# Up projection of a hybrid encoder layer: product 2 with joined matmuls of 512 columns and a sum of two halves

## The chip, the cores and the metric

The kernel runs on one core of a Trainium2 chip. The metric is the device time of one execution in microseconds (us); less is better.

## What is computed

One layer of a hybrid bidirectional encoder for 512 tokens of width 2048, all in float32. The part that matters here is the gated MLP at its end:

```python
xn = rms_norm(x, ffn_norm_g[l])
up = jnp.einsum("bsd,df->bsf", xn, w_up[l])          # 2048 -> 2 x 5632
up = depthwise_conv(up, ffn_dw_w[l], ffn_dw_b[l])    # width 3 over the tokens
gate, val = jnp.split(up, 2, axis=-1)
x = x + jnp.einsum("bsf,fd->bsd", jax.nn.silu(gate) * val, w_down[l])
```

Ahead of it stand an input projection with a convolution branch and an attention branch, and an output projection; behind it a final RMS norm.

## The kernel before

**Stages.** In order of time: the input projection with both branches (lines 374, 158 to 161), the output projection (158 to 161), the up projection (727 to 776), the down projection (882) and the final norm. This document is about the up projection, which runs from about 690 to 1555 us of the span. It is a loop of 44 rounds (`NF`), one for each block of 128 gate columns and 128 value columns.

**Seven products.** A round does not multiply the four quarters of its weights (A11, A12, A21, A22) with the two halves of the contraction and the two halves of the tokens in eight products, but forms sums of quarters and of activations beforehand and makes seven products of half the tokens (a Strassen-like scheme in the Winograd form). The products are named by a number `c` from 0 to 6 and run in the order `TURN = (3, 2, 4, 5, 1, 0, 6)`. So product 2 is the second to run. Its result is the one that is added to both halves of the value columns.

**Two parts of each number.** To keep float32's accuracy with the faster float32r matmuls, each operand is split in a high part (rounded) and a low part (the rest). A product of weights `hi`, `lo` and activations `mh`, `ml` is hi·mh + hi·ml + lo·mh, each over eight blocks of contraction (`U = 8`). In `comb[c][k]` a tile of 512 columns holds `mh` in its first 256 columns (`H = 256`) and `ml` in the other 256.

- Joined form (all products but 2): one matmul of `hi` with all 512 columns gives hi·mh in the first half of the PSUM bank and hi·ml in the second; one of `lo` with 256 columns adds lo·mh to the first half. That makes 8 matmuls of 512 and 8 of 256 columns. The two halves must be added afterwards, which `folded` does: ScalarE (ACT) copies the second half to SBUF, VectorE (DVE) adds the first. `FIRST` names the products that run their high part ahead of the low one; the others run the low part first.
- Product 2 uses `mm3` instead: three matmuls of 256 columns for each block, all into the first half of the bank. That makes 24 matmuls of 256 columns, and one copy by ACT (line 763) takes the result out.

**Banks.** Products 3, 4 and 1 accumulate one after another in the bank `pa`; ACT copies its state to other banks in between (`copied`, line 752). Product 4 can begin to add only when the copy of `pa` after product 3 is done; product 2, which has a bank `pc_` of its own, runs meanwhile.

**Around it.** For each product ACT rounds the raw weights to `whi` (line 131) and DVE makes `wlo` (line 132). Weights are made three products ahead (`AHEAD`), with four buffers for `whi` and `wlo` (`NW`) and nine for the raw weights (`NR`), which come over the SyncE (SP) queue; two of the seven weights in a round get a second quarter added by a transfer issued by GpSimd (POOL, line 687), two by DVE (lines 697 and 699). DVE and ACT also do the convolution of the round before: line 785 on ACT, two taps for the gate and two for the value on DVE (786 and 787), the silu (804) and the product (805). All instructions of an engine run in the order that a priority scheduler wrote out when the kernel was built; within a product, `pin` keeps the first matmul of a block in program order.

Of the kernel before, what the change touches and what calls it, by code (L numbers as in the profile page):

```python
# [12 lines left out]
AF = mybir.ActivationFunctionType  # L13
# [3 lines left out]
P = 128  # L17
D = 2048
S = 512
# [15 lines left out]
U = 8  # L35
# [5 lines left out]
H = S // 2  # L41
# [10 lines left out]
NEG = -1.0e30  # L52

TURN = (3, 2, 4, 5, 1, 0, 6)
FIRST = (3, 5, 0)
TURN2 = (3, 0, 4, 1, 2, 6, 5)
Q = D // 2 // S
TAIL = 4
# [16 lines left out]
def layer(ctx: ExitStack, tc: tile.TileContext, xT, xn, w_0, w_in, w_out, w_up, w_down, par, tab, g3, out):  # L75
    nc = tc.nc
# [8 lines left out]
    @contextmanager  # L85
    def shifted(by):

        at = tc.cur_priority
        tc.cur_priority = max(at + by, 0)
        yield  # L90
        tc.cur_priority = at + (tc.cur_priority - max(at + by, 0))

    def t2(name, dt=F32):
        return tp.tile([P, S], dt, tag="t2k", name=name)
# [23 lines left out]
    ps = psm.tile([P, S], F32, tag="mm", name="warm")  # L118
# [5 lines left out]
    def raw_unit(src, n):  # L124
        raw = t4([P, U * P], "raw")
        return raw, nc.sync.dma_start(raw[:, :n], src)

    def parts(raw, n):
        hi = wpool.tile([P, U * P], F32R, tag="whi", name="whi", bufs=NW)
        lo = wpool.tile([P, U * P], F32R, tag="wlo", name="wlo", bufs=NW)  # L130
        i = nc.scalar.activation(hi[:, :n], raw[:, :n], AF.Copy)  # L131
        j = nc.vector.tensor_sub(lo[:, :n], raw[:, :n], hi[:, :n].bitcast(F32))  # L132
        with tc.issue_after(j.ins), shifted(600):
            for _ in range(min(len(taps), TAPS)):
                taps.pop(0)()
        return hi, lo, i, j
# [3 lines left out]
        return parts(raw_unit(src, n)[0], n)[:2]  # L140

    tight, taps = [], []

    def mm3(ps, w, wk, mh, ml, start, stop, more=False):
        hi, lo = w[:2]
        a = slice(wk * P, (wk + 1) * P)
        i = nc.tensor.matmul(ps, hi[:, a], mh, start=start, stop=False, skip_group_check=more)  # L147
        if tight:
            pin(i)
        nc.tensor.matmul(ps, hi[:, a], ml, start=False, stop=False, skip_group_check=more)  # L150
        return nc.tensor.matmul(ps, lo[:, a], mh, start=False, stop=stop, skip_group_check=more)  # L151


    def group(ps, ws, ms, first, last):

# [10 lines left out]
    def tick(behind):  # L166
        for todo in (steps, asteps):
            while todo:
                try:
                    with tc.issue_after(behind.ins):  # L170
                        next(todo[0])
                    break
                except StopIteration:
                    todo.pop(0)
# [5 lines left out]
    def weights():  # L180
        at = weights.at
        weights.at += 1
        for i in range(at, min(at + 1 + FAR, len(plan))):
            if i in sums:
                sums.pop(i)()
        while len(made) < min(at + 1 + AHEAD, len(plan)):
            made.append(plan[len(made)]())
        return made[at]
# [85 lines left out]
    pin = tc.keep_in_program_order  # L274
# [33 lines left out]
    for u in range(2):  # L308
        raw, i = raw_unit(w_in[NC_ + 1, :, u * U * P:(u + 1) * U * P], U * P)
        pin(i)  # L310
        for t in range(2 * u, 2 * u + 2):
            for i in range(2):
                x = t4([P, D // 2], "xn")
                pin(nc.sync.dma_start(x, xn[t * P:(t + 1) * P, i * D // 2:(i + 1) * D // 2]))
                if t == 2 * u and i == 0:
                    w = parts(raw, U * P)
# [8 lines left out]
    for step in ORDER:  # L325
        i = next(a_ if step == "a" else q_)
# [242 lines left out]
    p, n = -1, 0  # L569
# [50 lines left out]
    comb = [[] for _ in range(7)]  # L620
# [104 lines left out]
    pd_, pb, pc_ = (psm.tile([P, S], F32, tag="mm", name="pu") for _ in range(3))  # L725
# [3 lines left out]
    def up(f, done):  # L729

        def product(c, ps, more):
            hi, lo = wt = weights()
            if c == 2:
                for k in range(U):
                    m = comb[c][k]
                    i = mm3(ps[:, :H], wt, k, m[:, :H], m[:, H:], k == 0, k == U - 1)
            else:
                turns = [(part, n, k) for part, n in ((lo, H), (hi, S))[::-1 if c in FIRST else 1]
                         for k in range(U)]
                if f == 0 and c == 3:  # L740
                    turns.sort(key=lambda a: a[2])
                for j, (part, n, k) in enumerate(turns):
                    i = nc.tensor.matmul(ps[:, :n], part[:, k * P:(k + 1) * P], comb[c][k][:, :n],  # L743
                                         start=j == 0 and not more, stop=j == 2 * U - 1, skip_group_check=more)
                    if j == 0 and tight:
                        pin(i)
            tick(i)
            done(TURN.index(c), i)

        def copied(to, ps):  # L750
            with shifted(-100):
                nc.scalar.activation(to, ps, AF.Copy)  # L752

        def folded(to, ps):
            nc.scalar.activation(to, ps[..., H:], AF.Copy)
            add(to, to, ps[..., :H])  # L756

        product(3, pa, False)
        tight[:] = [1] * (f > 0)
        copied(pd_, pa)  # L760
        product(2, pc_, False)
        w = t2("w")[:, :H]
        nc.scalar.activation(w, pc_[:, :H], AF.Copy)
        product(4, pa, True)
        copied(pe, pa)
        product(5, pd_, True)
        g = t2("g")
        folded(g[:, :H], pd_)
        product(1, pa, True)
        copied(pb, pa)  # L770
        product(0, pe, True)
        v = t2("vl")
        by = v.rearrange("p (i t) -> p i t", i=2)
        folded(by[:, 1], pa)
        folded(by[:, 0], pe)
        add(by, by, w.unsqueeze(1).broadcast_to([P, 2, H]))
        product(6, pb, True)
        folded(g[:, H:], pb)
        return g, v
# [14 lines left out]
    def hidden(f, done):  # L794
        g, v = up(f, done)

        def finish():
            nc.vector.tensor_mul(g, g, rstd2[0])
            a = conv3(g, f)
            yield  # L800
            nc.vector.tensor_mul(v, v, rstd2[0])
            b = conv3(v, NF + f)
            yield
            nc.scalar.activation(a, a, AF.Silu)
            nc.vector.tensor_mul(a, a, b)
            if f < NF - KEEP:
                nc.sync.dma_start(hd[f], a)
            else:
                hs[f] = a

        if f == NF - 1:
            steps.append(finish())
        else:
            for _ in finish():
                pass
# [47 lines left out]
    def four(first):  # L863

        if first:
            b = psa.tile([P, 2, S], F32, tag="sc", name="pd2")
            return [b[:, 0], b[:, 1]] + [psa.tile([P, S], F32, tag="tr", name="pd", bufs=2) for _ in range(2)]
        return [psm.tile([P, S], F32, tag="mm", name="pd") for _ in range(3)] + [psa.tile([P, S], F32, tag="po",
                                                                                         name="pd")]
# [108 lines left out]
    a = four(True)  # L978
# [18 lines left out]
    a = four(True)  # L997
# [74 lines left out]
```

## Time and profile before

| what | value |
|---|---|
| time, median of 3 runs | 1985.71 us (1985.69 to 1985.72) |
| time of the profiled execution | 1985.57 us |
| its span, first to last instruction | 1983.8 us |
| mean granted TensorE clock | 0.999 |
| 132 copies of a bank by ACT (line 752), mean | 580 ns |
| 573 splits by ACT (line 131) and by DVE (line 132), mean | 1058 and 1222 ns |

In the rows of the profile PE is TensorE's matmuls, PEld its weight loads, L743 is line 743 of the kernel before. A row of the timeline gives the start (us from the span's start), the time, engine, line, operation, output and inputs, tile sizes, how many were merged in the row, and in brackets the idle time before it with what ended it. A row of groups gives the count, then the busy time in us, the mean of one in ns, and the idle time in front. A row of waits gives who waited for whom, the us in total, how often, and the longest. Matmuls overlap: the next starts before the one before has ended.

### The profile page before, as it was taken

What the parts mean: (1) busy time and instruction counts of PE and PEld (TensorE: products, weight loads), DVE (VectorE), ACT (ScalarE), POOL (GpSimd) and SP (SyncE); (2) the same over time, 40 slices, a digit from 0 to 9 for tenths busy, and PEclk for the clock granted to TensorE, in tenths of its full rate; (3) what the DMA queues carried; (4) which work ended last, traced back from release to release, by engine and by line L of the source; (5) the groups of instructions that cost most, each with busy time, mean ns of one, the idle gap of its engine ahead of it and who ended that gap; (6) DMA issues with size and microseconds to landing.
All of it is one profiled execution on the core that took longest, in us unless ns stands there. A gap on an engine that the chain in (4) does not pass through costs nothing.

```text
span 1983.8 us, 28536 instructions
## 1 busy us (share of the span) xinstructions
PE 1969.9 (99%) x10525; PEld 1687.1 (85%) x10525; DVE 1602.7 (81%) x2318; ACT 1098.5 (55%) x1726; POOL 226.0 (11%) x310
## 2 busy tenths in 40 slices
PE   9999999999999999999999999999999999999998
PEld 7888888888788888989899898989898888888886
DVE  5987688788547888888888888888888898886765
ACT  7244424448525676666666666656666644554654
POOL 0111111111001111111111111111110400000000
PEclk9999999999999999999999999999999999999999
DMA  9776777676858889999999999999986977666663
GB/s 367 192 195 178 186 184 190 181 188 189 261 151 212 207 228 273 248 261 250 260 260 246 263 244 266 241 270 241 268 228 182 357 257 229 220 215 195 192 198 122
DMA packets 141821, 451.04 MB, mean 227 GB/s; under 512 B 15088, under 2 KB 23536, under 8 KB 140272
## 3 DMA queue, kind: packets, MB, share of 16 engines
q1 hardware_dynamic: 88880, 293.46, 43.8%
q0 software_dynamic: 42624, 148.92, 35.9%
q10 hardware_dynamic: 10176, 6.83, 1.1%
q8 instruction: 83, 1.36, 0.3%
q14 instruction: 58, 0.48, 0.1%
HBM read 430.27 MB, written 111.15 MB: 273 GB/s over the span
## 4 chain that ended last, share of the span: by engine, by line
PE 93%; DVE 3%; ACT 2%; issue 1%; DMA 1%; ACTq 0%; DVEq 0%
PE pu L743 37%; PE pd L882 21%; PE pj L161 6%; PE pj L158 6%; PE pj L159 6%; PE po L158 3%; PE po L161 3%; PE po L159 3%; PE pu L151 2%; PE pu L150 2%; PE pu L147 2%; PE po L530 1%; PE trp L516 1%; ACT s L506 1%; PE pj L374 1%
## 5 line engine op out<-in xcount | busy, mean ns | idle before, releaser
L131 ACT ACTIVATE whi<-raw 128x1024 fp32r<-128x1024 f32 x573 | 601.7, 1058 | 561.5 <-PE pj L159 171.7
L132 DVE TENSOR_TENSOR wlo<-raw,whi 128x1024 fp32r<-128x1024 f32 x573 | 696.4, 1222 | 253.8 <-ACT whi L131 209.1
L743 PE MATMUL pu<-xc,whi 128*128 128x512 f32 x2112 | 505.6, 391 | 0.1
L743 PEld LDWEIGHTS pu<-xc,whi 128*128 128x128 f32 x2112 | 388.2, 188 | 75.3 <-DVE xc L626 0.3
L882 PE MATMUL pd<-whi,ho 128*128 128x512 f32 x1232 | 305.1, 389 | 0.1
L743 PEld LDWEIGHTS pu<-xc,wlo 128*128 128x128 f32 x2112 | 274.4, 191 | 10.3
L743 PE MATMUL pu<-xc,wlo 128*128 128x256 f32 x2112 | 282.3, 283 | 0.0
L882 PEld LDWEIGHTS pd<-whi,ho 128*128 128x128 f32 x1232 | 231.2, 188 | 48.6 <-DVE vl L756 0.5
L158 PE MATMUL pj<-xh,whi 128*128 128x512 f32 x608 | 241.3, 397 | 0.0
L159 PE MATMUL pj<-xl,whi 128*128 128x512 f32 x608 | 237.4, 390 | 0.0
L400 DVE SCALAR_TENSOR_TENSOR y<-ch,prm,y 128x500 f32<-128x500 f32 (+14 forms) x240 | 177.2, 742 | 5.1
L882 PE MATMUL pd<-wlo,ho 128*128 128x512 f32 x616 | 165.1, 389 | 0.0
L161 PE MATMUL pj<-xh,wlo 128*128 128x512 f32 x608 | 151.0, 390 | 0.0
L752 ACT ACTIVATE pu<-pu 128x512 f32<-128x512 f32 x132 | 76.5, 580 | 121.7 <-PE pu L743 121.5
L158 PEld LDWEIGHTS pj<-xh,whi 128*128 128x128 f32 x608 | 114.1, 188 | 26.3 <-issue 3.6
L882 PEld LDWEIGHTS pd<-wlo,ho 128*128 128x128 f32 x616 | 115.7, 188 | 24.0
L161 PEld LDWEIGHTS pj<-xh,wlo 128*128 128x128 f32 x608 | 114.1, 188 | 23.6
L159 PEld LDWEIGHTS pj<-xl,whi 128*128 128x128 f32 x608 | 114.3, 188 | 23.0 <-issue 0.2
L213 POOL DMA_DIRECT2D ws<-in_w_down x88 | 79.7, 905 | 372.4 <-DMA raw<-in_w_up 130.9
L687 POOL DMA_DIRECT2D raw<-in_w_up x88 | 78.0, 887 | 280.2 <-DVE wlo L132 152.6
L147 PE MATMUL pu<-xc,whi 128*128 128x256 f32 x352 | 99.6, 283 | 0.0
L150 PE MATMUL pu<-xc,whi 128*128 128x256 f32 x352 | 99.6, 283 | 0.0
(190 smaller groups left out, 2318.4 us busy)
## 6 DMA issues: line engine op xcount, KB each, us to landing
raw<-in_w_up SPq DMA_DIRECT2D x220, 512.0 KB, 5.4
ws<-in_w_down POOLq DMA_DIRECT2D x132, 512.0 KB, 6.2
raw<-in_w_up POOLq DMA_DIRECT2D x88, 512.0 KB, 7.6
raw<-ws SPq DMA_DIRECT2D x88, 512.0 KB, 4.3
raw<-in_w_in SPq DMA_DIRECT2D x76, 512.0 KB, 5.1
raw<-in_w_down SPq DMA_DIRECT2D x66, 512.0 KB, 4.5
ws<-ws POOLq DMA_DIRECT2D x44, 512.0 KB, 6.0
raw<-in_w_out SPq DMA_DIRECT2D x32, 512.0 KB, 5.2
```

The costliest lines, as they stand in the source:

```text
L131: i = nc.scalar.activation(hi[:, :n], raw[:, :n], AF.Copy)
L132: j = nc.vector.tensor_sub(lo[:, :n], raw[:, :n], hi[:, :n].bitcast(F32))
L147: i = nc.tensor.matmul(ps, hi[:, a], mh, start=start, stop=False, skip_group_check=more)
L150: nc.tensor.matmul(ps, hi[:, a], ml, start=False, stop=False, skip_group_check=more)
L158: nc.tensor.matmul(ps, hi, mh, start=first and k == 0, stop=False)
L159: nc.tensor.matmul(ps, hi, ml, start=False, stop=False)
L161: i = nc.tensor.matmul(ps, lo[:, wk * P:(wk + 1) * P], mh, start=False, stop=last and k == len(ws) - 1)
L213: nc.gpsimd.dma_start(wsum[c][k], w_down[k, {1: A21, 2: A11, 4: A11, 6: A12}[c]], accum_op=ALU.add, max_dma_last_dim=ROW)
L400: nc.vector.scalar_tensor_tensor(y[:, a:b], h[:, a + j - PAD:b + j - PAD], prm[:, o:o + 1], y[:, a:b], op0=ALU.mult, op1=ALU.add)
L687: nc.gpsimd.dma_start(a[c], w_up[f, q2], accum_op=ALU.add)
L743: i = nc.tensor.matmul(ps[:, :n], part[:, k * P:(k + 1) * P], comb[c][k][:, :n], start=j == 0 and not more, stop=j == 2 * U - 1, skip_grou ...
L882: m = nc.tensor.matmul(ps[i], h[:, o + t * P:o + (t + 1) * P], w[:, d], start=start and not more and kind == 0 and j == 0, stop=stop and k ...
```

## The change

Product 2 joins `FIRST` and takes the joined form like the others, high part first; `mm3` is gone, and so is the branch that called it. Its result then has two halves, and `folded` replaces the copy.

```diff
-FIRST = (3, 5, 0)
+FIRST = (3, 2, 5, 0)
...
-    def mm3(ps, w, wk, mh, ml, start, stop, more=False):
-        hi, lo = w[:2]
-        a = slice(wk * P, (wk + 1) * P)
-        i = nc.tensor.matmul(ps, hi[:, a], mh, start=start, stop=False, skip_group_check=more)
-        if tight:
-            pin(i)
-        nc.tensor.matmul(ps, hi[:, a], ml, start=False, stop=False, skip_group_check=more)
-        return nc.tensor.matmul(ps, lo[:, a], mh, start=False, stop=stop, skip_group_check=more)
...
         def product(c, ps, more):
             hi, lo = wt = weights()
-            if c == 2:
-                for k in range(U):
-                    m = comb[c][k]
-                    i = mm3(ps[:, :H], wt, k, m[:, :H], m[:, H:], k == 0, k == U - 1)
-            else:
-                turns = ...
+            turns = [(part, n, k) for part, n in ((lo, H), (hi, S))[::-1 if c in FIRST else 1]
+                     for k in range(U)]
...
         product(2, pc_, False)
         w = t2("w")[:, :H]
-        nc.scalar.activation(w, pc_[:, :H], AF.Copy)
+        folded(w, pc_)
```

`folded` was there before:

```python
        def folded(to, ps):
            nc.scalar.activation(to, ps[..., H:], AF.Copy)
            add(to, to, ps[..., :H])
```

The line numbers of the changed kernel are 10 to 15 lower behind the edits.

More of the change, by code (lines that the diff above doesn't have):

```diff
@@ L732, in product @@
             hi, lo = wt = weights()
-            if c == 2:
-                for k in range(U):
-                    m = comb[c][k]
-                    i = mm3(ps[:, :H], wt, k, m[:, :H], m[:, H:], k == 0, k == U - 1)
-            else:
[L738 to L746, printed above, removed]
+            turns = [(part, n, k) for part, n in ((lo, H), (hi, S))[::-1 if c in FIRST else 1]
+                     for k in range(U)]
+            if f == 0 and c == 3:
+                turns.sort(key=lambda a: a[2])
+            for j, (part, n, k) in enumerate(turns):
+                i = nc.tensor.matmul(ps[:, :n], part[:, k * P:(k + 1) * P], comb[c][k][:, :n],
+                                     start=j == 0 and not more, stop=j == 2 * U - 1, skip_group_check=more)
+                if j == 0 and tight:
+                    pin(i)
             tick(i)
```

## The prediction

> **What bounds the kernel now.** I read the page first: its busy times and its chain of work that ended last.
>
> ```profile
> span 1983.8 us, 28536 instructions
> PE 1969.9 (99%) x10525; PEld 1687.1 (85%) x10525; DVE 1602.7 (81%) x2318; ACT 1098.5 (55%) x1726; POOL 226.0 (11%) x310
> ...
> PE 93%; DVE 3%; ACT 2%; issue 1%; DMA 1%; ACTq 0%; DVEq 0%
> ```
>
> TensorE (PE) is the chain for 93% of the span. The change touches only the up projection, so I asked for the busy times of one round of it (one of 44, from one start of product 2 to the next) and of the stretch in which all the steady rounds lie, and for the waits of that stretch, first on PE and then on DVE.
>
> ```profile
> core 0: us, PE busy (x) PEld busy (x) DVE busy (x) ACT busy (x) POOL busy (x), PEclk, DMA share, GB/s
> 1049.15:1068.73 19.58, 19.58 (x123) 17.64 (x121) 16.95 (x22) 12.30 (x19) 3.21 (x4) 1.00 0.94 252
> 700.00:1540.00 840.00, 839.84 (x5148) 756.25 (x5147) 727.09 (x913) 529.75 (x777) 130.40 (x163) 1.00 0.94 248
> ...
> PE st L269 <- DVE acc L231: 0.2, 1, 0.2
> ...
> DVE wlo L132 <- ACT whi L131: 102.8, 85, 1.9
> ```
>
> PE is busy for all of the 19.58 us of a round, at a granted clock of 1.00; in 840 us it waits once, for 0.2 us. So this stage is as long as PE's own list of matmuls, and a nanosecond off that list is a nanosecond off the kernel, as long as nothing else becomes late. Next to it stand DVE with 16.95 of 19.58 us and the DMA engines at 0.94: the two that could.
>
> **PE's list.** The timeline of PE over the same round, and a later cut of it that begins behind the first eight matmuls of a joined block:
>
> ```profile
> 1048.20 1.11 PE L743 MATMUL pu<-xc,wlo 128*128 128x256 f32 x8
> 1049.15 0.28 PE L147 MATMUL pu<-xc,whi 128*128 128x256 f32 x1
> 1049.27 0.28 PE L150 MATMUL pu<-xc,whi 128*128 128x256 f32 x1
> ...
> 1051.91 0.28 PE L151 MATMUL pu<-xc,wlo 128*128 128x256 f32 x1
> 1052.03 1.12 PE L743 MATMUL pu<-xc,wlo 128*128 128x256 f32 x8
> 1052.99 3.82 PE L743 MATMUL pu<-xc,whi 128*128 128x512 f32 x16
> 1056.64 2.08 PE L743 MATMUL pu<-xc,wlo 128*128 128x256 f32 x16
> 1058.56 3.82 PE L743 MATMUL pu<-xc,whi 128*128 128x512 f32 x16
> 1062.21 2.08 PE L743 MATMUL pu<-xc,wlo 128*128 128x256 f32 x16
> ...
> 1054.83 1.98 PE L743 MATMUL pu<-xc,whi 128*128 128x512 f32 x8
> ```
>
> What counts is start to start, since the 0.28 us of one matmul lie over the next. Product 2 now has 24 matmuls of 256 columns, from 1049.15 to 1052.03: 2.88 us, 0.12 each. A joined product has 8 of 512 and 8 of 256 columns. The columns are the same (24 x 256 = 8 x 512 + 8 x 256); only the number of matmuls and weight loads falls, from 24 to 16.
>
> The price of the 16 depends a little on what stands before them. In the changed kernel product 2 runs its high part behind the low part of product 3, then its low part. A high eight that follows low ones takes 1054.83 - 1052.99 = 1.84 us; the second eight of that block, behind high ones, takes 1056.64 - 1054.83 = 1.81. A low eight behind high ones takes 1049.15 - 1048.20 = 0.95; inside low ones 0.96 (1052.03 to 1052.99). So the new product 2 takes 1.84 + 0.95 = 2.79 us; in nanoseconds the same starts give 1841 + 953 = 2794, against 2880: **0.086 us less in a round**. The bounds are the mean of the six joined products, (19.58 - 2.88) / 6 = 2.783, 0.097 less, and 0.08 from the rounding of the rows. I take 0.086, since its neighbours are those of the new place. Product 4 behind it still begins with its low part behind low ones, and product 3 before it is untouched.
>
> Here a page speaks against the size of this gain. The Trainium skill, "TensorE: Matmul & The Clock Gate", section "Back-to-back issue gap", gives a warm matmul its columns over 2.4 GHz plus about 2.5 ns; by that, dropping eight matmuls at equal columns would save 8 x 2.5 = 20 ns a round, 0.9 us in 44. The trace differs: 0.12 us for 256 columns and 0.227 for 512 leave about 13 ns a matmul beside the columns.
>
> **44 rounds:** 44 x 0.086 = 3.8 us. The first round has its own order, still waits for its operands, and may give 0.1 to 0.2; counted as an ordinary one it errs by a tenth.
>
> **What is added.** Product 2's result has two halves now, so its copy to SBUF becomes `folded`: ACT copies one half, DVE adds the other. Groups of the stage:
>
> ```profile
> L763 ACT ACTIVATE w<-pu 128x256 f32<-128x256 f32 x44 | 16.1, 365 | 0.0
> L755 ACT ACTIVATE vl<-pu 128x256 f32<-128x256 f32 x88 | 33.3, 380 | 40.4 <-PE pu L743 40.4
> L756 DVE TENSOR_TENSOR g<-g,pu 128x256 f32<-128x256 f32 x88 | 36.4, 414 | 1.2 <-ACT g L755 1.2
> ```
>
> On ACT nothing but the half changes (365 against 380 ns at most). On DVE one add of 0.414 us a round is new, 18.2 us in all. DVE's slack is 19.58 - 16.95 = 2.6 us a round, so the sum fits; but DVE works in order, and the add waits for ACT, which waits for product 2. So I walked the stretch in which it stands. In the built kernel DVE's order there is: tap on vl (L786), **the new add**, tap on vl (L787), split (`wlo`), L805, L699, split, add to g, split, split; before, the first split stood ahead of L787, L805 behind L699, and the add to g one split later.
>
> ```profile
> 1052.75 0.74 DVE L786 SCALAR_TENSOR_TENSOR uy<-vl,fwn,uy 128x511 f32<-128x511 f32 x1
> 1053.41 1.22 DVE L132 TENSOR_TENSOR wlo<-raw,whi 128x1024 fp32r<-128x1024 f32 x1
> 1054.55 0.74 DVE L787 SCALAR_TENSOR_TENSOR uy<-vl,fwn,uy 128x511 f32<-128x511 f32 x1
> 1055.21 1.22 DVE L699 TENSOR_TENSOR raw<-raw 128x1024 f32<-128x1024 f32 x1
> 1056.35 0.68 DVE L805 TENSOR_TENSOR uy<-uy 128x512 f32<-128x512 f32 x1
> 1057.55 2.36 DVE L132 TENSOR_TENSOR wlo<-raw,whi 128x1024 fp32r<-128x1024 f32 x2 [0.53 <-ACT whi L131]
> 1059.83 0.41 DVE L756 TENSOR_TENSOR g<-g,pu 128x256 f32<-128x256 f32 x1
> 1062.17 1.23 DVE L132 TENSOR_TENSOR wlo<-raw,whi 128x1024 fp32r<-128x1024 f32 x1 [1.93 <-ACT whi L131]
> ...
> 1050.12 0.58 ACT L752 ACTIVATE pu<-pu 128x512 f32<-128x512 f32 x1
> ...
> 1052.16 1.06 ACT L131 ACTIVATE whi<-raw 128x1024 fp32r<-128x1024 f32 x1 [0.72 <-ACT uy L785]
> ...
> 1056.46 2.01 ACT L131 ACTIVATE whi<-raw 128x1024 fp32r<-128x1024 f32 x2 [0.85 <-DVE raw L699]
> ...
> 1060.60 0.58 ACT L752 ACTIVATE pu<-pu 128x512 f32<-128x512 f32 x1 [1.86 <-PE pu L743]
> 1061.09 1.05 ACT L131 ACTIVATE whi<-raw 128x1024 fp32r<-128x1024 f32 x1
> ```
>
> Start to start a tap takes 0.66 us, a split 1.14, L805 0.60 and the add to g 0.33. Product 2 ends near 1051.94 now; ACT then copies its half behind the `whi` that ends by 1053.2 at the latest, so by 1053.6, while the add's turn on DVE comes at 1053.41: a wait of 0.2 at most (none, if that `whi` starts earlier, as it may, since the buffer it reuses is free when product 2's high part is done). Without the wait: L787 at 1053.74, split 1054.40, L805 1055.54, L699 1056.14. The `whi` that needs L699 started 1.25 behind it (1055.21 to 1056.46), so now at 1057.39, and its split at 1058.48, **0.93 later than before**; then g at 1059.62, the next split at 1059.95, done near 1061.1. The split after that waited to 1062.17 for a `whi` which itself waits for PE (1060.60): DVE had 1.93 us to spare there and still has about 1.0. So the delay dies within the round. Its victims have cover: the split that is 0.93 late is for product 6, whose low part begins at 1062.21 + 0.96 = 1063.17; it is done at 59.7, 3.5 us ahead. Loads whose buffer DVE frees start up to 1.1 us later. In the waits of DVE and ACT over this stretch none is ended by a transfer, so loads land with room; POOL's order is unchanged, SP's only where its loads meet the stage's ends.
>
> One cover shrinks: the copy of `pa` (1050.12 + 0.58 = 1050.70) must be done before product 4 adds to that bank, at 1052.03 before, 1051.94 now; 1.2 us are left.
>
> **Sum.** The profiled execution took 1985.57 us, 0.14 under the median of the runs, 1985.71. 1985.57 - 3.8 = 1981.8, on the median's footing **1981.9 us**, 0.19% less. A change of 0.2% is 3.97 us, about what a measurement of this kernel can tell from no change; my sum lies just inside.
>
> **The rivals.**
> *No gain, or part of it.* PE streams as many columns as before; if time went by columns alone, nothing would be saved: 1985.7. Against it: the round's own rows price both shapes. The DMA engines cannot hold the round at 19.58 either: at a share of 0.94 their work fills 18.4 us of it. Chance 0.12, with all gains under 0.075 us a round; half of the gain would give 1983.8. By the page named above, "TensorE: Matmul & The Clock Gate" of the Trainium skill, it would be 1984.8.
> *Slower: DVE becomes the round.* Mechanism: the new add, in order and behind ACT, pushes the split behind L699 past what 1.93 us of idle can take back. Place: the `whi` after 1060.60. My walk uses 0.9 of it. If the late part were over 1.93 us, each round would grow by the excess e, first eating the 3.5 us of product 6's cover; against before it is slower once e is above 0.086 us. For e = 0.3 the time is 1985.7 + 44 x (0.3 - 0.086) - 3.5 = 1991.6. For it: DVE goes from 16.95 to some 17.3 of 19.49 us and waits for ACT 85 times in the stage. Against it: a whole microsecond is left in the walk. Chance 0.12.
> *More gain.* The high eight follows only eight low ones, not sixteen; if it ran at 1.81, a round would save 0.12, and the kernel 5.3: 1980.4. Chance 0.06.
>
> **How the numbers follow.** The forecast, 0.075 to 0.1 us a round (1981.3 to 1982.4), has 0.70. The range 1980.4 to 1983.8 adds the greater gain and the upper half of the smaller ones: 0.70 + 0.06 + 0.06, about 0.8. Faster by over 0.2% needs 0.090 us a round: some 0.28 of the 0.70, and the 0.06: 0.34. Within 0.2%: the other 0.42 and the 0.12 of no gain: 0.54. Slower: 0.12.
>
> **What would show it.** Right: product 2 as eight matmuls of 512 and eight of 256 columns in 2.79 us, a round of 19.49 us, PE still busy throughout, some 10173 matmuls in place of 10525, a DVE add `w<-w,pu` x44 of 0.41 us, the idle before the split after 1060.60 down from 1.93 to about 1.0, the one behind L699 up from 0.53 to about 1.1. Wrong: PE waiting for `wlo` in the stage, or for ACT's copy of `pa` (the slower rival); a high eight of 1.81 behind low ones; a round of 19.56 or more with PE busy.

## The result, and the profile after

The changed kernel takes **1982.03 us** (median of 17 runs, 1981.46 to 1982.94) against 1985.69 us for the one before in the same comparison (17 runs, 1985.27 to 1986.07): 3.66 us less, a ratio of **0.9981** with a 95% interval of 0.9975 to 0.9988. So it is faster: the two sets of runs do not touch. The gain is just below the 0.2% that the prediction took as about the least that can be told from no change. The profiled execution took 1981.86 us.

The page of the changed kernel, its busy times and its chain:

```profile
span 1980.1 us, 27714 instructions
PE 1965.8 (99%) x10173; PEld 1668.0 (84%) x10173; DVE 1617.2 (82%) x2362; ACT 1098.3 (55%) x1726; POOL 226.0 (11%) x310
...
PE 93%; ACT 2%; DVE 2%; DMA 1%; issue 1%; ACTq 0%; SPq 0%; DVEq 0%
```

There are 352 matmuls and weight loads fewer (8 in each of 44 rounds), 44 instructions more on DVE, and PE is the chain for 93% as before. What was to be seen next is whether PE is still busy for the whole of the stage. The busy times of the steady rounds (the window ends at 1536 us, since the stage is shorter now):

```profile
core 0: us, PE busy (x) PEld busy (x) DVE busy (x) ACT busy (x) POOL busy (x), PEclk, DMA share, GB/s
700.00:1536.00 836.00, 835.90 (x4804) 738.02 (x4804) 741.09 (x956) 529.38 (x777) 129.97 (x162) 1.00 0.94 250
```

PE is busy for 835.90 of 836.00 us, and the view of waits has no row for PE in this window. The time therefore came out of PE's list itself, which the timeline of PE shows over one round, from one start of product 2 to the next:

```profile
1046.82 1.11 PE L728 MATMUL pu<-xc,wlo 128*128 128x256 f32 x8
1047.77 2.00 PE L728 MATMUL pu<-xc,whi 128*128 128x512 f32 x8
1049.61 2.08 PE L728 MATMUL pu<-xc,wlo 128*128 128x256 f32 x16
1051.52 3.82 PE L728 MATMUL pu<-xc,whi 128*128 128x512 f32 x16
...
1067.26 2.00 PE L728 MATMUL pu<-xc,whi 128*128 128x512 f32 x8
```

Line 728 is line 743 of the kernel before. Product 2 is the row of eight with 512 columns at 1047.77 and the first half of the row of sixteen that follows. The round is 1067.26 - 1047.77 = 19.49 us long. The starts in nanoseconds give 19.580 us before and 19.493 after in each of the 43 steady rounds, 3.7 us in all, and 0.17 us less in the first round. From its first to its last matmul the stage went from 864.25 to 860.36 us, 3.89 less. Of the span 3.70 is left: the stage began 0.26 us later in this execution, behind a part of the program that the change does not touch, and what lies behind the stage was 0.06 us shorter.

On DVE the same stretch as in the prediction's walk, from its timeline (L771 and L772 are the taps, L741 the add of `folded`, L790 the product, L689 the add of a quarter):

```profile
1051.37 0.74 DVE L771 SCALAR_TENSOR_TENSOR uy<-vl,fwn,uy 128x511 f32<-128x511 f32 x1
1052.03 0.41 DVE L741 TENSOR_TENSOR w<-w,pu 128x256 f32<-128x256 f32 x1
1052.37 0.74 DVE L772 SCALAR_TENSOR_TENSOR uy<-vl,fwn,uy 128x511 f32<-128x511 f32 x1
1053.03 1.22 DVE L132 TENSOR_TENSOR wlo<-raw,whi 128x1024 fp32r<-128x1024 f32 x1
1054.16 0.68 DVE L790 TENSOR_TENSOR uy<-uy 128x512 f32<-128x512 f32 x1
1054.76 1.22 DVE L689 TENSOR_TENSOR raw<-raw 128x1024 f32<-128x1024 f32 x1
1057.10 1.23 DVE L132 TENSOR_TENSOR wlo<-raw,whi 128x1024 fp32r<-128x1024 f32 x1 [1.12 <-ACT whi L131]
1058.24 0.41 DVE L741 TENSOR_TENSOR g<-g,pu 128x256 f32<-128x256 f32 x1
1058.58 1.22 DVE L132 TENSOR_TENSOR wlo<-raw,whi 128x1024 fp32r<-128x1024 f32 x1
1060.71 1.23 DVE L132 TENSOR_TENSOR wlo<-raw,whi 128x1024 fp32r<-128x1024 f32 x1 [0.92 <-ACT whi L131]
```

The new add starts at 1052.03 with no idle time in front. The split behind L689 starts 5.73 us after the tap (1051.37 to 1057.10), against 4.80 before (1052.75 to 1057.55): 0.93 later. The idle time in front of it is 1.12 (0.53 before), and the one in front of the split that had 1.93 to spare is 0.92. The waits of DVE in the window, and then the group of the new add, say the same for the whole stage:

```profile
DVE wlo L132 <- ACT whi L131: 84.6, 84, 1.1
```

```profile
L741 DVE TENSOR_TENSOR w<-w,pu 128x256 f32<-128x256 f32 x44 | 18.2, 413 | 0.7 <-ACT w L740 0.7
```

DVE waited for `whi` 102.8 us in 840 before, at most 1.9 at a time; now 84.6 in 836, at most 1.1. That is 2.40 us a round before and 1.97 now, so the 0.41 us of the new add came out of that idle time. One add in 44 waited for ACT, for 0.7 us.

### The profile page after: what moved, and what is told of

The parts are those of the page before. It is cut to its first block, busy times and chain, and to the rows that moved or that the text cites. A ratio compares the mean times of both kernels' runs of the same rounds, so it can differ in the third digit from the quotient of the medians.

```text
span 1980.1 us, 27714 instructions
## 1 busy us (share of the span) xinstructions
PE 1965.8 (99%) x10173; PEld 1668.0 (84%) x10173; DVE 1617.2 (82%) x2362; ACT 1098.3 (55%) x1726; POOL 226.0 (11%) x310
## 4 chain that ended last, share of the span: by engine, by line
PE 93%; ACT 2%; DVE 2%; DMA 1%; issue 1%; ACTq 0%; SPq 0%; DVEq 0%
PE pu L728 43%; PE pd L867 21%; PE pj L151 6%; PE pj L148 6%; PE pj L149 6%; PE po L148 3%; PE po L151 3%; PE po L149 3%; PE po L520 1%; PE trp L506 1%; ACT s L496 1%; PE pj L364 1%; DMA x<-in_xT 1%; DVE s L488 1%; ACT s L493 0%
## 5 line engine op out<-in xcount | busy, mean ns | idle before, releaser
L728 PE MATMUL pu<-xc,whi 128*128 128x512 f32 x2464 | 593.6, 391 | 0.0
L728 PEld LDWEIGHTS pu<-xc,whi 128*128 128x128 f32 x2464 | 451.4, 188 | 86.7 <-DVE xc L616 0.4
L728 PEld LDWEIGHTS pu<-xc,wlo 128*128 128x128 f32 x2464 | 319.2, 191 | 13.7
L728 PE MATMUL pu<-xc,wlo 128*128 128x256 f32 x2464 | 324.2, 283 | 0.0
L203 POOL DMA_DIRECT2D ws<-in_w_down x88 | 79.6, 904 | 299.4 <-DMA ws<-in_w_down 115.6
L200 POOL DMA_DIRECT2D ws<-ws x44 | 23.4, 531 | 321.6 <-PE pj L151 109.2
L200 POOL DMA_DIRECT2D ws<-in_w_down x44 | 23.1, 524 | 321.5 <-PE pj L151 178.1
```

The costliest lines, as they stand in the source:

```text
L200: behind(nc.gpsimd.dma_start(wsum[c][k], a), ins)
L203: nc.gpsimd.dma_start(wsum[c][k], w_down[k, {1: A21, 2: A11, 4: A11, 6: A12}[c]], accum_op=ALU.add, max_dma_last_dim=ROW)
```

## The experiments

The theory: the gain is PE's list alone, one round being 0.086 us shorter because eight matmuls less are issued, and the add is hidden in DVE's spare time. Its rivals: the add costs something that the shorter list pays for; the order of high and low parts, not the number of matmuls, sets the gain; and DVE is close to being the round.

### The add without the joined matmuls

```diff
 # in the kernel before, behind ACT's copy of product 2 to w
+        add(w, w, pc_[:, :H])
```

> The kernel before with the new DVE add alone: product 2 keeps its 24 matmuls of 256 columns, ACT's copy is followed by a DVE add that reads the same half of the bank once more (so product 2 counts twice in the values). Theory (the gain is PE's own list of matmuls, the add is hidden): a round stays 19.58 us and the time 1985.7 us, within 1 us. Rival (DVE becomes the round): the add shows, up to 44 x 0.33 = 14.5 us more, about 2000 us, and PE waits for wlo.

Measured: 1985.91 us (10 runs, 1985.58 to 1986.14), ratio 1.0 with an interval of 0.9991 to 1.001. Rounds of 19.580 us, as before. The stretch, and then DVE's waits in it:

```profile
700.00:1536.00 836.00, 835.85 (x5121) 752.56 (x5120) 737.45 (x951) 526.81 (x773) 129.69 (x161) 1.00 0.92 250
```

```profile
DVE wlo L132 <- ACT whi L131: 88.1, 84, 1.1
```

PE is busy for 835.85 of 836 us, and DVE's longest wait for `whi` falls to 1.1 us, as in the changed kernel. The add alone moves DVE just as the change does, and it costs nothing.

### The joined matmuls without the add

```diff
 # in the changed kernel
-        folded(w, pc_)
+        nc.scalar.activation(w, pc_[..., :H], AF.Copy)
```

> The changed kernel without its DVE add: product 2 runs 8 matmuls of 512 and 8 of 256 columns, but only the first half of the bank is copied out (the high weights times the low activations of product 2 are left out of the result). Theory (PE's list alone): a round of 19.49 us and 1982.0 us, as the changed kernel. Rival (the add eats a part of the gain): faster than 1982.0, by 44 times what the add costs. Rival (the gain came from the new order of DVE and ACT, not from the matmuls): DVE has its old order here, so 1985.7.

Measured: 1982.16 us (10 runs, 1981.49 to 1982.87), ratio 0.9982 (0.9973 to 0.9991); rounds of 19.493 us. DVE's timeline has its old order back, the split ahead of the second tap, and with it the old idle times:

```profile
1053.09 1.22 DVE L132 TENSOR_TENSOR wlo<-raw,whi 128x1024 fp32r<-128x1024 f32 x1
1054.23 0.74 DVE L772 SCALAR_TENSOR_TENSOR uy<-vl,fwn,uy 128x511 f32<-128x511 f32 x1
1054.89 1.21 DVE L689 TENSOR_TENSOR raw<-raw 128x1024 f32<-128x1024 f32 x1
1056.03 0.68 DVE L790 TENSOR_TENSOR uy<-uy 128x512 f32<-128x512 f32 x1
1057.23 2.36 DVE L132 TENSOR_TENSOR wlo<-raw,whi 128x1024 fp32r<-128x1024 f32 x2 [0.52 <-ACT whi L131]
1059.51 0.41 DVE L741 TENSOR_TENSOR g<-g,pu 128x256 f32<-128x256 f32 x1
1061.77 1.23 DVE L132 TENSOR_TENSOR wlo<-raw,whi 128x1024 fp32r<-128x1024 f32 x1 [1.85 <-ACT whi L131]
```

The two experiments add up: the matmuls carry the whole gain, the add nothing. Taking 0.9 us of spare time from DVE or giving it back changes no round.

### Product 5 cut up as product 2 was

```diff
 # in the kernel before
-            if c == 2:
+            if c in (2, 5):
 ...
-                    i = mm3(ps[:, :H], wt, k, m[:, :H], m[:, H:], k == 0, k == U - 1)
+                    i = mm3(ps[:, :H], wt, k, m[:, :H], m[:, H:], k == 0 and not more, k == U - 1, more)
```

> The kernel before with product 5, too, as 24 matmuls of 256 columns (result unchanged; its two halves are still added). Theory (the price is PE's starts: 120 ns a matmul of 256 columns behind another, 113 for the first behind a high one): 5's part of the round goes from 1813 + 953 to 24 x 120 - 7 = 2873 ns, and the low eight behind it from 960 to 960: 107 ns a round more, 19.687 us, 44 x 0.107 = 4.7 us, 1990.4 us. By the price of equal columns (no fixed cost of a matmul): 1985.7.

Measured: 1990.56 us (10 runs, 1990.15 to 1990.75), ratio 1.0024 (1.0014 to 1.0034); rounds of 19.687 us, 0.107 longer. PE's timeline, product 5 with its 24 matmuls:

```profile
1055.05 2.00 PE L743 MATMUL pu<-xc,whi 128*128 128x512 f32 x8
1056.89 0.28 PE L147 MATMUL pu<-xc,whi 128*128 128x256 f32 x1
1057.01 0.28 PE L150 MATMUL pu<-xc,whi 128*128 128x256 f32 x1
...
1059.65 0.28 PE L151 MATMUL pu<-xc,wlo 128*128 128x256 f32 x1
1059.77 1.12 PE L743 MATMUL pu<-xc,wlo 128*128 128x256 f32 x8
```

It takes 1059.77 - 1056.89 = 2.88 us by these rows and 2.873 in nanoseconds, against 2.766 in the joined form. The number of passages from low parts (256 columns) to high parts (512 columns) stays what it was, three in a round, so this is the price of the eight matmuls by themselves: 0.107 us at equal columns, 13 ns each. Each brings a weight load of its own, and no run parts the two. In the change the eight gave only 0.086, because product 2 also brought a new passage; what that costs is the next experiment.

### Every product with its high part first

```diff
 # in the changed kernel
-FIRST = (3, 2, 5, 0)
+FIRST = (3, 2, 4, 5, 1, 0, 6)
```

> The changed kernel with the high part first in all seven products, so that a round has seven high blocks behind low ones in place of four: the same 112 matmuls, only their order differs. Theory (a high eight costs 1.841 us behind low ones and 1.813 behind high ones, a low eight 0.953 behind high ones and 0.960 behind low ones): three more passages each way, 3 x (28 - 7) = 63 ns a round more, 19.557 us a round, 1982.0 + 2.8 = 1984.8 us. Rival (the price goes by the counts of matmuls alone): 1982.0.

Measured: 1984.24 us (10 runs, 1984.02 to 1984.66), ratio 0.9992 (0.9983 to 1.0002), where 1984.8 was expected; rounds of 19.553 us where 19.557 was expected. PE's timeline:

```profile
1051.80 2.00 PE L728 MATMUL pu<-xc,whi 128*128 128x512 f32 x8
1053.64 1.11 PE L728 MATMUL pu<-xc,wlo 128*128 128x256 f32 x8
1054.60 2.00 PE L728 MATMUL pu<-xc,whi 128*128 128x512 f32 x8
1056.44 1.11 PE L728 MATMUL pu<-xc,wlo 128*128 128x256 f32 x8
```

Each product takes some 2.79 us, its high part 1.84 (1051.80 to 1053.64). The same matmuls in another order cost 0.060 us a round more. Seven times in a round a high part follows a low one here, four times in the changed kernel, so a passage and its return cost 0.020 us. PE does not wait in either. That settles the rival of more gain: every high eight behind low ones takes 1.84, whether eight or sixteen low ones stand ahead.

### How much more DVE can take: two, four and eight extra adds

Each of the three adds work to DVE that the result does not use, behind the fold of product 2:

```diff
 # in the changed kernel
-        w = t2("w")[:, :H]
+        wt = t2("w")
+        w = wt[:, :H]
         folded(w, pc_)
+        for _ in range(2):          # 4, 8
+            add(wt[:, H:], w, w)
```

> The changed kernel with two more DVE adds of 256 columns a round behind the new one (into an unused half of a tile, result unchanged), 0.34 us each start to start. Theory (DVE has about 0.9 us a round to spare in the changed kernel, the idle before the split that waits for the copy after product 1): hidden, 1982.0 us, that idle down from 0.92 to about 0.25. Rival (DVE is already on the edge): 44 x 0.68 = 30 us more, about 2012.

Measured: 1982.37 us (10 runs, 1982.07 to 1982.82), ratio 0.9983 (0.9974 to 0.9992), rounds of 19.493 us. The adds are hidden, but not where it was expected: on DVE's timeline the idle time of 0.92 us fell to 0.58 and not to about 0.25, because the one of 1.12 us behind L689 fell as well, to 0.60.

> The changed kernel with four more DVE adds a round (result unchanged). Theory (DVE becomes the round only when its work and the bubble that no work covers fill 19.49 us): two adds brought DVE's busy time from 17.28 to 18.03 us a round, so four make 18.8; one of them now stands behind the add of a quarter to the weights and covers a part of the bubble there, of which about 0.4 us stay; 19.2 us, under 19.49: hidden, 1982 us. Rival, the prediction's walk (1.36 us of adds against 0.92 us of spare idle, each excess paid in every round): 44 x 0.44 - 3.5 = 16 us more, 1998 us.

Measured: 1982.2 us (10 runs, 1981.9 to 1982.73), ratio 0.9982 (0.9973 to 0.9992), rounds of 19.493 us. The stretch, and then DVE's waits with four adds:

```profile
700.00:1536.00 836.00, 835.92 (x4805) 738.16 (x4804) 798.39 (x1127) 533.58 (x777) 130.62 (x163) 1.00 0.94 250
```

```profile
DVE wlo L132 <- ACT whi L131: 27.4, 78, 0.5
```

DVE is busy for 798.39 of 836 us, its longest wait for `whi` is 0.5, and no round is longer. The rival's price, had its walk gone on (four adds are 1.3 us in front of the split, and 0.92 was left), did not come. DVE's timeline has the same two splits:

```profile
1057.91 2.36 DVE L132 TENSOR_TENSOR wlo<-raw,whi 128x1024 fp32r<-128x1024 f32 x2 [0.46 <-ACT whi L131]
1060.51 1.23 DVE L132 TENSOR_TENSOR wlo<-raw,whi 128x1024 fp32r<-128x1024 f32 x1 [0.24 <-ACT whi L131]
```

The adds also fill the 1.12 us in front of the split behind L689, which the walk had kept (0.46 is left), and the scheduler wrote out another order around them.

> The changed kernel with eight more DVE adds a round (result unchanged). Theory: DVE's work is 17.28 + 8 x 0.375 = 20.3 us a round, over 19.49, so DVE becomes the round: 43 x 0.8 less the 3.5 us of cover = 31 us more, about 2013 us, with PE waiting for wlo. Rival (PE's list bounds whatever DVE does): 1982 us.

Measured: 1996.73 us (4 runs, 1996.1 to 1998.15), ratio 1.0057 (1.0042 to 1.0072). The second and third rounds take 20.566 and 19.971 us, the steady ones 19.763. The stretch, and then from the views of waits those of the weight loads in it and one of PE behind it:

```profile
700.00:1536.00 836.00, 834.79 (x4736) 724.28 (x4735) 831.75 (x1278) 508.95 (x765) 129.20 (x161) 1.00 0.94 247
```

```profile
PEld pu L728 <- DVE vl L741: 16.1, 40, 0.7
PEld pu L728 <- DVE wlo L132: 1.0, 1, 1.0
...
PE pd L870 <- DVE vl L741: 2.0, 1, 2.0
```

Now DVE is the round: busy for 831.75 of 836 us, with no wait for `whi` left in the window. But what PE waits for is mostly not `wlo`, as the expectation and the prediction's slower rival had it: that came once, in the second round (1.0 us). From then on, once a round and for 0.4 us on average, a weight load waits for DVE's fold of product 1 out of the bank `pa`, which product 3 of the next round needs. The timeline of PE shows it as a longer block of sixteen, 3.92 us from start to start where the changed kernel has 3.66:

```profile
1048.66 4.08 PE L728 MATMUL pu<-xc,whi 128*128 128x512 f32 x16
1052.58 1.11 PE L728 MATMUL pu<-xc,wlo 128*128 128x256 f32 x8
```

The stage grew by 12.4 us (860.36 to 872.80), and the late DVE reaches past it: a matmul of the down projection (L870) waits another 2.0 us for a fold. Together these are nearly all of the 14.7 us. The expected 2013 was too much because it charged 0.375 us for an add: by the rows of the two windows DVE's busy time grew from 17.28 us a round in the changed kernel (741.09 x 19.493 / 836) to 19.66 here (831.75 x 19.763 / 836), 0.30 for each of the eight.

## Why the prediction was right

It forecast 1981.9 us, and 1982.03 was measured. The mechanism is the one that was forecast. That the time came within 0.13 us is in part luck, since the runs of this one kernel spread over 1.5 us.

- **Product 2 in 2.79 us.** Confirmed within a nanosecond: the high eight takes 1841 ns and the low eight 952, 2793 in all where the prediction had 2794. A round is 0.0865 us shorter. The prices were read off joined products that already stood in the trace. Their neighbours were the same but for the low matmuls ahead, eight in place of sixteen, and that changed nothing; so they held.
- **44 rounds.** 43 steady ones gave 3.72 us, the first 0.17, within its 0.1 to 0.2. Of the 3.89 in the stage 3.70 shows in the span, as told with the result.
- **The add is hidden.** Confirmed twice: alone it changes no round (19.580), and its absence changes none (19.493).
- **The walk on DVE.** The 0.93 us came out as 0.93, the 1.1 as 1.12, the 1.0 left over as 0.92. The wait of 0.2 at most for ACT did not occur in the steady rounds: in the round shown ACT copies its half from 1050.90 and the add's turn comes at 1052.03. Once in the stage it was 0.7.
- **No gain.** It did not happen. Equal columns do not cost equal time: eight matmuls are worth 0.107 us at equal columns, 13 ns each, and two starts of 256 columns against one of 512 give the same, 2 x 120 - 226.7 = 13.3 ns. By the Trainium skill, "TensorE: Matmul & The Clock Gate", section "Back-to-back issue gap", the isolated gap of a warm matmul has about 2.5 ns beside its columns, which would make an estimate of 20 ns for the eight; the section does not give this formula for a stream in which each matmul loads its own weights, as here. The runs gave 13 ns a matmul, and the measurement decides.
- **Slower, by DVE.** The mechanism exists, as the run with eight adds shows, but its place and its point were wrong. With the change's own, five adds a round fitted and nine did not, so the change would have had to bring more than five, not one whose lateness passes 1.93 us; and what is late in the steady rounds is the fold that frees `pa`, not `wlo`. The step of this rival that failed is the assumption that DVE's order and the idle time behind L699 stay as they are while more is put in front.
- **More gain.** It did not happen either: product 2's high eight took 1.84, and with all parts high first no high eight took 1.81 behind low ones.

## What to carry to other kernels

When one engine is busy without a gap, price a new list of its instructions from starts of the same shapes with the same neighbours; a row's own duration (0.28 us for a matmul that takes 0.12) would have misled. At equal columns fewer, wider matmuls saved a fixed price each here (13 ns, between 256 and 512 columns), and changing width back and forth cost a little of it again, so blocks of one width belong together. To learn how much room a second engine has, add work to it until the round grows: idle time summed over a round (19.49 - 17.28 = 2.2 us) showed the room better than the one gap that a walk reached (0.92), since four adds took 1.3 us and fitted, and eight took 2.4 and did not.

## What the runs showed that was not expected

The passage between the two widths has a price of its own. The eight matmuls of 512 columns behind those of 256 start 233, 236, 229, 232, 230, 228, 226 and 227 ns apart, where 226.7 is the mean inside a run of them: about 28 ns more, spread over the first five. The first step back to 256 columns is 7 ns shorter than their 120. What causes it stays open. The runs show that it does not depend on whether eight or sixteen narrow ones stand ahead, and the profile has no wait of PE there. The change of weights from low to high part alone does not bring it: in the kernel before, product 2 changes both ways at one width, and its 24 matmuls start 120 ns apart throughout.
